# Second scan pass: vn copied ahead of vs behind the fifth level's copies, output sums issued behind the fourth level's mask

## The chip, the cores and the metric

One core of a Trainium2 chip runs the whole program. The metric is the device time of one execution in microseconds (us). Three executions of the kernel before gave 2560.66, 2562.65 and 2566.15 us; the median is 2562.65.

## The reference

One layer of a flow-matching backbone: a modulated RMS norm, then side by side a gated DeltaNet in both directions (4 heads of 128) and a gated spatial MLP, one input and one output projection, a residual add, and a squared-ReLU MLP. 128 context tokens and 2048 latent tokens are computed. The change touches the DeltaNet scan of the second (backward) direction. Cut to what matters:

```python
def gated_delta_chunked(q, k, v, g, beta, s0):
    ...
    a_mat = jnp.where(strict, jnp.einsum('bnhcd,bnhsd->bnhcs', k_beta, k) * decay, 0.0)
    sol = lax.linalg.triangular_solve(a_mat + jnp.eye(DN_CHUNK, dtype=f32), rhs,
                                      left_side=True, lower=True, unit_diagonal=True)
    ...
    def step(S, xs):
        qd, kd, u_c, w_c, qk_c, gl = xs
        v_new = u_c - jnp.einsum('bhck,bhkv->bhcv', w_c, S)
        o = jnp.einsum('bhck,bhkv->bhcv', qd, S) + jnp.einsum('bhcs,bhsv->bhcv', qk_c, v_new)
        S = S * jnp.exp(gl)[..., None, None] + jnp.einsum('bhck,bhcv->bhkv', kd, v_new)
        return S, o

def delta_bidir(q, k, v, g2, beta2, s0):
    o_f, s_f = gated_delta_chunked(q, k, v, g2[:, :, 0], beta2[:, :, 0], s0[:, 0])
    ...
    return o_f + flip(o_b), jnp.stack([s_f, s_b], axis=1)

def mixer(h, s0, n_chunks, w_in_l, conv_l, a_log_l, dt_bias_l, o_norm_l, ws_l, bs_l, w_out_l):
    proj = h @ w_in_l
    ...
    o_a = rmsnorm(o_a, o_norm_l) * jax.nn.silu(gate.reshape(B, T, H_A, DV))
    ...
    return out @ w_out_l, s_new
```

## The kernel before

The program has five stages on TensorE (PE). An input projection runs to about 490 us. A first (forward) scan pass over 17 chunks of 128 tokens, units 0 to 16, ends at about 860. The second (backward) pass, units 17 to 33, follows to about 1205 (one unit is about 21 us). Then come the two products of the MLP. Large products are made of three reduced-precision products each, lines L241, L242 and L243 (a high and a low part of each operand).

A unit has two halves. Its **prep** inverts a triangular matrix of 128 by 128 for each of four heads: from the loaded tiles KK and QK it makes AH (ACT, L1080) and X, and then goes through five levels s = 2, 4, 8, 16, 32. A level is a product AH·Y (L1109), a mask on VectorE (DVE) that makes P (L1113), a pair of products (L1122, L1124), and copies of Y and X on ScalarE (ACT, L1125 and L1126). Behind the second level's copies stands QK times the decay E (DVE, L1129). Then the two blocks of 64 are joined (L1141, copy P on ACT L1142, L1148 and L1150), and a last correction gives R (DVE, L1162) and T (ACT, L1171). The prep of one unit runs ahead of its scan, and two units' levels interleave.

The **scan** has four steps, written with a helper quad() that issues four products, one for each head (all at L1026):

1. S·kT into vt (DVE, L1183); S·qT into o (ACT, L1175);
2. T·vt into a PSUM tile p; vs = p times a column (DVE, L1196); vn = p (ACT, L1198);
3. vs·kt, and S updated from it (DVE, L1212);
4. vn·QK, and two output sums: o from o and the forward pass's output of (DVE, L1231), then o plus the product (DVE, L1233).

The output o is then normed (ACT L1363; DVE L1366 to L1371, called rr and o in the trace) and transposed on PE (L1384, o and the spatial half ob) into oH (ACT, L1387) and oL (DVE, L1388). The output projection, the **fills**, is 48 products for each unit: 24 for each half n of the columns, in PSUM tiles pj or pm. At its end stand tmp (DVE, L1407) and x + tmp (DVE, L1408), and for t > 8 further steps for the MLP (norm, transposes L888, stores from opH and opL, L902 to L909).

What runs when is set by a list of events with times in units; sorted by time, they issue their instructions. Each engine's queue is in that order but for what a scheduler may move. Two rules constrain it: emit() ties each fill behind the fourth last event of a chain or prep, and calm() ties the DVE and ACT instructions of a function behind the last instruction that level_done() has marked on their engine (on DVE the masks and the join's Y, on ACT the copies of X):

```python
        def level_done(n):
            x = tc.nc.cur_bb.bb.instructions[-1]
            urgent[x.engine].append(x)
        def calm(f, lag=0):
            start = here()
            f()
            for x in tc.nc.cur_bb.bb.instructions[start:]:
                if x.engine in urgent and len(urgent[x.engine]) > lag:
                    tc.add_manual_dep(x, urgent[x.engine][-1 - lag].name, ...)
```

All DMAs of the pass are issued by SyncE (SP) in one queue: loads (KK L1031, QK L1035 by qk_load, kt and vt L1043, kT and qT L1041) and stores. QK has three buffers; the PSUM tiles pd of prep and scan rotate through four.

Of the kernel before, what the change touches and what calls it, by code (L numbers as in the profile page):

```python
# [13 lines left out]
ALU = mybir.AluOpType  # L14
# [7 lines left out]
NT = 17  # L22
# [21 lines left out]
BT = 1  # L44
# [20 lines left out]
def hybrid_step(  # L65
# [7 lines left out]
    V, A, G, T = nc.vector, nc.scalar, nc.gpsimd, nc.tensor  # L73
# [137 lines left out]
    def here():  # L211
        return len(tc.nc.cur_bb.bb.instructions)
# [82 lines left out]
    with ExitStack() as ph:  # L295
# [496 lines left out]
        for bi in range(len(BLOCKS)):  # L792
# [6 lines left out]
            at = {e: n for n, e in enumerate(order)}  # L799
            tile_of = {}  # L800
            for n, (gi, h) in enumerate(order):
                u = us[n] if bi == 0 and n < 3 else feature_tile(blk, bi, gi, h)
# [157 lines left out]
    with ExitStack() as ph:  # L960
# [8 lines left out]
        def pd():  # L969
            return psd.tile([P, 4, P], F32, tag="d", name="pd", bufs=4)  # L970
# [10 lines left out]
        def q32(tag, bufs=1, pool=None):  # L981
            return (pool or dl).tile([P, 4, P], F32, tag=tag, name=tag, bufs=bufs)
# [24 lines left out]
# [6 lines that stand above are left out]
                    tc.add_manual_dep(x, urgent[x.engine][-1 - lag].name, mybir.DependencyInfo(  # L1013
                        mybir.DependencyClass.NoSync, mybir.DependencyReason.DATA), reason="order")

        def unit(t, d):

            u = {}
# [5 lines left out]
            def quad(p, lhs, rhs):  # L1024
                for h in range(H):
                    T.matmul(p[:, h, :], lhs[:, h, :], rhs[:, h, :], start=True, stop=True)  # L1026
# [21 lines left out]
            @prep.append  # L1048
            def _():
                e = s32("E")  # L1050

                def decay():
                    for h in range(H):
                        A.activation(e[:, h, :], u["gb"][:, h, :], AF.Abs, scale=-1.0, bias=col(gcol, h))
                    A.activation(e, e, AF.Exp, scale=-1.0)

                calm(decay, 2) if d else decay()
                es = s32("Es")
                G.affine_select(out=es, in_=e, pattern=[[0, 4], [-sg, P]], compare_op=ALU.is_gt, fill=0.0,
                                base=0, channel_multiplier=sg)  # L1060
                G.affine_select(out=e, in_=e, pattern=[[0, 4], [sg, P]], compare_op=ALU.is_ge, fill=0.0,
                                base=0, channel_multiplier=-sg)
                u["Es"], u["E"] = es, e
# [126 lines left out]
            @scan.append  # L1190
            def _():
                p = pd()
                quad(p, u["T"], u["vt"])
                u["vs"] = q32("vs", 1)
                cols = eglg[:, t, d * 4 : d * 4 + 4].unsqueeze(2).to_broadcast([P, 4, P])
                V.tensor_tensor(out=u["vs"], in0=p, in1=cols, op=ALU.mult)  # L1196
                u["vn"] = q32("vn", BT)
                A.copy(u["vn"], p)  # L1198

            @scan.append  # L1200
            def _():
# [16 lines left out]
            @scan.append  # L1218
            def _():
                p = pd()  # L1220
                quad(p, u["QK"], u["vn"])
                of = u["of"].rearrange("p (h d) -> p h d", h=H) if d else None
                if u["s"] is None:
                    u["o"] = o = q32("o", 2)
                    if d == 0:
                        A.copy(o, p)
                    else:
                        V.tensor_tensor(out=o, in0=p, in1=of, op=ALU.add)
                else:
                    o = u["o"]  # L1230
                    V.scalar_tensor_tensor(out=o, in0=o, scalar=-0.5, in1=of if d else p, op0=ALU.mult, op1=ALU.add)  # L1231
                    if d:
                        V.tensor_tensor(out=o, in0=o, in1=p, op=ALU.add)  # L1233
                if d == 0:
                    store(out=of_d[t * P : (t + 1) * P, :].rearrange("p (h d) -> p h d", h=H), in_=o)

# [108 lines left out]
        def o_loads(u):  # L1345
            t = u["t"]
            u["of"], u["ga"] = w512("of"), w512("ga")
            load(out=u["of"], in_=of_d[t * P : (t + 1) * P, :])
            load(out=u["ga"], in_=gate_d[t * P : (t + 1) * P, :])
# [74 lines left out]
        def at(time, fn, kind=None):  # L1424
            events.append((time, len(events), fn, kind))

        def spread(t0, t1, steps, kind):
            for j, st in enumerate(steps):
                at(t0 + (t1 - t0) * (j + 0.5) / len(steps), st, kind)

        def scan_step(i, f):
            def g():
                u = units[i]
                if "s" not in u:
                    u["s"] = None if i in (0, NT) else units[i - 1]["sn"] if i not in (1, NT + 1) else u["s0"]
                f()
            return g

        def after(i):

            d = 0 if i == 0 else 1
            store(out=new_state[0, 0, d].rearrange("h k v -> k h v"), in_=units[i]["sn"])

        def state_load(i):

            s0 = fpart("s0").rearrange("p (h d) -> p h d", h=H)
            load(out=s0, in_=state_delta[0, 0, 0 if i == 0 else 1].rearrange("h k v -> k h v"))
            units[i + 1]["s0"] = s0

        def noted(name, f):  # L1450

            start = here()
            f()
            done[name] = tc.nc.cur_bb.bb.instructions[start:]

        def after_weights(f, names, engines):

            start = here()
            f()
            for name in names:  # L1460
                behind(name, start, engines)

        p2, p3 = WINDOWS[:8], WINDOWS[8:]
        for i, u in enumerate(units):
            w = p2 if i <= NT else p3
            at(i - 3 if i > 1 else -12.1, lambda i=i, u=u: noted(("kk", i), u["prep_loads"]))
            at(i - 3 if i > 1 else -11.1, lambda i=i, u=u: after_weights(
                u["qk_load"], (("kk", 1),) if i < 2 else (), (mybir.EngineType.SP,)))
            at(i - 1, lambda i=i, u=u: after_weights(u["scan_loads"], LATER.get(i, ()), (mybir.EngineType.SP,)))
            u["prep"][:2] = [lambda i=i, f=f: after_weights(f, AHEAD_OF.get(i, ()), (mybir.EngineType.Activation,  # L1470
                                                                                    mybir.EngineType.DVE))
                             for f in u["prep"][:2]]
            n = len(u["prep"])
            for j, st in enumerate(u["prep"]):
                at(i - w[0] + (j + 0.5) * (w[0] - w[1]) / n if i or j > 9 else -11.6 if j < 2
                   else 0.2 * j - 8.15, st, "prep")
            for j, f in enumerate(u["scan"]):
                behind_join = 0.12 if j == 2 and i > NT else 0.0
                at(i + w[2] + (w[3] - w[2]) * (j + 0.5) / 4 + behind_join, scan_step(i, f), "chain")
            if i in (0, NT):  # L1480
                at(i - 1, lambda i=i: state_load(i))
                at(i + w[2] + (w[3] - w[2]) * 0.7, lambda i=i: after(i))
            if i >= NT:
                at(i, lambda u=u: o_loads(u))
                first, second = o_steps(u)
                spread(i + p3[4], i + p3[5], first, "fill")
                spread(i + p3[6], i + p3[7], second, "fill")
                if u["t"] > 8:
                    st = h2_steps(u["t"], pj, fraw, w512, fpart, fhalf, lambda u=u: u["x2"])
                    spread(i + p3[8], i + p3[9] + 0.2, st[:5], "fill")  # L1490
                    spread(i + p3[9] + 0.2, i + p3[9] + 2.1, [lambda f=f: calm(f) for f in st[5:]], None)
# [73 lines left out]
    def add(out, a, b, op=ALU.add):  # L1565
        V.tensor_tensor(out=out, in0=a, in1=b, op=op)  # L1566
# [199 lines left out]
    def sums(i, k, r):  # L1766
        if i == 1:
            add(r[0], r[1], r[0], ALU.subtract)
            store(out=t_d[5, k], in_=r[0])
            add(r[1], r[2], r[1], ALU.subtract)  # L1770
            store(out=t_d[7, k], in_=r[1])
        elif i == 5:
            add(r[1], r[1], r[0], ALU.subtract)
            store(out=t_d[6, k], in_=r[1])
        else:
            add(r[0], r[0], r[1], ALU.subtract)
            store(out=t_d[4, k], in_=r[0])
# [192 lines left out]
    for j, t in enumerate(range(8, -1, -1)):  # L1970
        st = h2_steps(t, bank, lambda: w512("junk"), w512)
        p = 10 + 19 * j // 2
# [7 lines left out]
    for p, (o, n, b) in enumerate(seq):  # L1980
        u = units[n]
# [130 lines left out]
```

## Time and profile before

| what | us |
|---|---|
| median of 3 executions | 2562.65 |
| profiled execution, its time | 2561.29 |
| profiled execution, span of the trace | 2559.5 |
| PE busy | 2531.2 |
| DVE busy | 1829.7 |
| ACT busy | 1258.6 |
| DMA queue of all loads and stores, mean share of 16 engines | 70.3% |

The granted clock of TensorE is 0.999 over the run. The span is the trace from its first to its last instruction; "idle" in a view is the time in which an engine waited before a line, with what released it. The chain of work that ended last is PE for 88% of the span, DMA 5%, DVE 4% and ACT 2%. For a short wait in a stage with a PE that is almost always busy, the waits of PE and the timeline of that stage are the views to use.

### The profile page before, as it was taken

To read this page: it belongs to the slowest core of one execution; us is meant where nothing else is said; L and a number is where in the kernel's file an instruction comes from. 1 tells how busy PE (TensorE), PEld (TensorE's weight loads), DVE (VectorE), ACT (ScalarE), POOL (GpSimd) and SP (SyncE) were. 2 spreads that over 40 slices of the span, in tenths; PEclk is the share of its full clock that TensorE was granted. 3 is DMA by queue.
4 is the path that set the end of the run, shared out by engine and by line. 5 is a ranking of instruction groups with operands and counts; after the bars stand their busy time and mean duration, and the time that the engine had idled before them with its cause. 6 is when DMAs were issued, how large, how long until landed. Compare 5 with 4: busy or idle time off the path is not lost.

```text
span 2559.5 us, 44412 instructions
## 1 busy us (share of the span) xinstructions
PE 2531.2 (99%) x15268; PEld 2135.2 (83%) x15268; DVE 1829.7 (71%) x3790; ACT 1258.6 (49%) x3119; POOL 228.2 (9%) x448
## 2 busy tenths in 40 slices
PE   9999999999999999999999999999999999999998
PEld 5999999788888788788888888888888888888887
DVE  5867746776666878886678877777675557784875
ACT  4755556554554767763455544444342433243442
POOL 3112212211101111110000000000000000000000
PEclk9999999999999999999999999999999999999999
DMA  8977747744445657785867789665489979786673
GB/s 286 308 222 207 210 120 230 261 155 153 149 145 161 210 176 256 263 302 190 304 207 233 241 286 348 191 180 172 145 272 371 340 265 327 251 262 208 225 261 110
DMA packets 503912, 588.66 MB, mean 230 GB/s; under 512 B 36148, under 2 KB 298588, under 8 KB 500102
## 3 DMA queue, kind: packets, MB, share of 16 engines
q1 hardware_dynamic: 503686, 585.82, 70.3%
q8 instruction: 120, 1.97, 0.3%
q14 instruction: 106, 0.87, 0.1%
HBM read 406.01 MB, written 179.67 MB: 229 GB/s over the span
## 4 chain that ended last, share of the span: by engine, by line
PE 88%; DMA 5%; DVE 4%; ACT 2%; issue 1%; SPq 0%; POOL 0%; POOLq 0%; DVEq 0%; ACTq 0%
PE f L241 16%; PE f L243 16%; PE f L242 16%; PE pj L241 7%; PE pj L243 7%; PE pj L242 7%; PE pd L1026 5%; PE pm L241 2%; PE pm L243 1%; PE pm L242 1%; PE pt L625 1%; DMA raw<-in_w_mod_dram 1%; PE pt L584 1%; DMA QK<-qk_d 1%; DMA raw<-in_w_ff_dram 1%
## 5 line engine op out<-in xcount | busy, mean ns | idle before, releaser
L241 PE MATMUL f<-hop,zH 128*128 128x512 f32 (+1 forms) x976 | 376.2, 386 | 1.2 <-ACT zH L1572 1.2
L242 PE MATMUL f<-hop,zH 128*128 128x512 f32 (+1 forms) x976 | 376.1, 386 | 0.0
L243 PE MATMUL f<-hop,zL 128*128 128x512 f32 (+1 forms) x976 | 376.1, 386 | 0.0
L241 PE MATMUL f<-hop,wH 128*128 128x512 f32 x896 | 349.5, 391 | 1.2 <-ACT p L1645 1.0
L242 PE MATMUL f<-hop,wH 128*128 128x512 f32 x896 | 348.7, 389 | 0.0
L243 PE MATMUL f<-hop,wL 128*128 128x512 f32 x896 | 347.1, 389 | 0.0
L1572 ACT CAST zH<-zraw 128x512 fp32r<-128x512 f32 x240 | 146.9, 620 | 294.6 <-DMA zraw<-s_d 89.6
L241 PEld LDWEIGHTS f<-hop,zH 128*128 128x128 f32 x976 | 183.4, 188 | 38.6 <-ACT zH L1572 1.8
L243 PEld LDWEIGHTS f<-hop,zL 128*128 128x128 f32 x976 | 183.4, 188 | 37.0 <-DVE zL L1566 0.4
L242 PEld LDWEIGHTS f<-hop,zH 128*128 128x128 f32 x976 | 183.4, 188 | 36.9 <-issue 0.2
L1566 DVE TENSOR_TENSOR zL<-zraw,zH 128x512 fp32r<-128x512 f32 x240 | 163.0, 687 | 66.9 <-ACT zH L1572 51.5
L241 PEld LDWEIGHTS f<-hop,wH 128*128 128x128 f32 x896 | 168.2, 188 | 36.8 <-ACT p L1645 2.0
L243 PEld LDWEIGHTS f<-hop,wL 128*128 128x128 f32 x896 | 168.2, 188 | 35.2
L242 PEld LDWEIGHTS f<-hop,wH 128*128 128x128 f32 x896 | 168.3, 188 | 34.5
L241 PE MATMUL pj<-kH,wH 128*128 128x386 f32 (+2 forms) x568 | 190.6, 338 | 1.7 <-ACT junk L601 1.1
L243 PE MATMUL pj<-kH,wL 128*128 128x386 f32 (+2 forms) x568 | 189.7, 335 | 0.0
L242 PE MATMUL pj<-kL,wH 128*128 128x386 f32 (+2 forms) x568 | 189.4, 335 | 0.0
L184 POOL TENSOR_TENSOR r<-rsq,nhalf 128x1 f32<-128x1 f32 (+1 forms) x37 | 23.4, 634 | 1380.4 <-DVE rsq L183 1380.4
L571 DVE SCALAR_TENSOR_TENSOR cv<-pj,vec,cv 128x384 f32<-128x384 f32 (+2 forms) x164 | 86.9, 539 | 52.4 <-ACT cv L568 51.0
L1572 ACT CAST wH<-s 128x512 fp32r<-128x512 f32 x96 | 59.4, 621 | 123.3 <-DVE s L1566 116.9
L241 PEld LDWEIGHTS pj<-kH,wH 128*128 128x128 f32 x568 | 107.1, 189 | 5.1 <-issue 2.4
L202 DVE TENSOR_TENSOR wL<-raw,wH 128x512 fp32r<-128x512 f32 x120 | 81.2, 684 | 38.6 <-ACT wH L201 35.5
(423 smaller groups left out, 5788.1 us busy)
## 6 DMA issues: line engine op xcount, KB each, us to landing
zraw<-z_d SPq DMA_DIRECT2D x212, 256.0 KB
raw<-in_w_ff_dram SPq DMA_DIRECT2D x192, 256.0 KB
hop<-hop_d SPq DMA_DIRECT2D x28, 1024.0 KB
z_d<-c SPq DMA_DIRECT2D x96, 256.0 KB
zraw<-s_d SPq DMA_DIRECT2D x96, 256.0 KB
raw<-in_w_mod_dram SPq DMA_DIRECT2D x80, 256.0 KB
r<-in_w_ff_dram SPq DMA_DIRECT2D x80, 256.0 KB
s_d<-s SPq DMA_DIRECT2D x64, 256.0 KB
```

The costliest lines, as they stand in the source:

```text
L184: G.tensor_tensor(out=out, in0=t[:np_, :n], in1=nhalf[:np_, :n], op=ALU.pow)
L202: V.tensor_tensor(out=lo, in0=raw, in1=f32(h), op=ALU.subtract)
L241: T.matmul(ps, lh, rh, start=first and i == 0, stop=False, skip_group_check=more)
L242: T.matmul(ps, lh, rl, start=False, stop=False, skip_group_check=more)
L243: T.matmul(ps, ll, rh, start=False, stop=last and i == n - 1, skip_group_check=more)
L571: V.scalar_tensor_tensor(out=cv[:, o : o + m], in0=ps[:, s + sh : s + sh + m], scalar=convw[:, w, j : j + 1], in1=cv[:, o : o + m], op0=AL ...
L584: T.transpose(pq[:, i * P : (i + 1) * P], u["x2"][:, i * P : (i + 1) * P], ident)
L625: T.matmul(ps[:, i * P : (i + 1) * P], kTt[:, i * P : (i + 1) * P], rhs[:, i * P : (i + 1) * P], start=True, stop=True)
L1026: T.matmul(p[:, h, :], lhs[:, h, :], rhs[:, h, :], start=True, stop=True)
L1566: V.tensor_tensor(out=out, in0=a, in1=b, op=op)
L1572: A.copy(h, src)
```

## The change

Three edits, all on the second pass (d = 1). In the scan's second step vn is now made before vs, and with calm(), so behind the last marked copy of X. In the fourth step the two output sums stand in a function and are tied with calm(), behind the last marked mask. The scan's events are issued a little later: the second step by 0.1 units, the third by 0.12 (as before), the fourth by 0.03.

```diff
@@ scan, step 2 @@
+                u["vn"] = q32("vn", BT)
+                if d:
+                    calm(lambda: A.copy(u["vn"], p))
                 V.tensor_tensor(out=u["vs"], in0=p, in1=cols, op=ALU.mult)
-                u["vn"] = q32("vn", BT)
-                A.copy(u["vn"], p)
+                if d == 0:
+                    A.copy(u["vn"], p)
@@ scan, step 4 @@
-                    V.scalar_tensor_tensor(out=o, in0=o, scalar=-0.5, in1=of if d else p, op0=ALU.mult, op1=ALU.add)
-                    if d:
-                        V.tensor_tensor(out=o, in0=o, in1=p, op=ALU.add)
+
+                    def sums():
+                        V.scalar_tensor_tensor(out=o, in0=o, scalar=-0.5, in1=of if d else p, op0=ALU.mult,
+                                               op1=ALU.add)
+                        if d:
+                            V.tensor_tensor(out=o, in0=o, in1=p, op=ALU.add)
+
+                    calm(sums) if d else sums()
@@ events @@
-                behind_join = 0.12 if j == 2 and i > NT else 0.0
-                at(i + w[2] + (w[3] - w[2]) * (j + 0.5) / 4 + behind_join, scan_step(i, f), "chain")
+                shift = {1: 0.1, 2: 0.12, 3: 0.03}.get(j, 0.0) if i > NT else 0.0
+                at(i + w[2] + (w[3] - w[2]) * (j + 0.5) / 4 + shift, scan_step(i, f), "chain")
```

The lines behind the edits have larger numbers in the kernel after: vs is L1199 there (L1198 is vn in both), S's update L1215, the sums L1236 and L1239, the o copies L1395 and L1396, and tmp and x + tmp are L1415 and L1416.

The next rows are ACT's order in unit 26, before. An 8x32 form of Y and X is the fifth level's pair of copies (two rows), and E, fraw and opH belong to other steps.

```order
1119 L1054 ACTIVATE E<-gb,gcol 128x128 x4
1120 L868 ACTIVATE fraw,ss_15495<-x 128x512
1121 L1055 ACTIVATE E<-E 128x512
1122 L1198 COPY vn<-pd 128x512
1123 L1387 CAST oH<-pj 128x512
1124 L1125 CAST Y<-pd 128x8x32
1125 L1126 CAST X<-pd 128x8x32
1126 L1125 CAST Y<-pd 128x64x4
```

The same place on ACT, after:

```order
1122 L1054 ACTIVATE E<-gb,gcol 128x128 x4
1123 L1055 ACTIVATE E<-E 128x512
1124 L1395 CAST oH<-pj 128x512
1125 L1125 CAST Y<-pd 128x8x32
1126 L1126 CAST X<-pd 128x8x32
1127 L1198 COPY vn<-pd 128x512
1128 L1125 CAST Y<-pd 128x64x4
1129 L1126 CAST X<-pd 128x64x4
```

vn has moved behind oH and the fifth level's copies, and ahead of those of the next unit's second level.

On DVE in the same unit, before (P with sm_186 is the fifth level's mask; opL and y belong to the MLP's steps; the numbers count the rows of the queue from the program's start):

```order
1356 L1129 TENSOR_TENSOR QK<-QK,E 128x512
1357 L1408 TENSOR_TENSOR x<-x,tmp 128x512
1358 L1366 TENSOR_TENSOR r_16639<-rq 128x4
1359 L1231 SCALAR_TENSOR_TENSOR o<-o,of 128x512
1360 L1369 SCALAR_TENSOR_TENSOR rr<-rr,rq 128x4
1361 L1371 SCALAR_TENSOR_TENSOR o<-o,rr,ga 128x128 x4
1362 L1113 TENSOR_TENSOR P_5794<-pd,sm_186 128x8x32
1363 L1113 TENSOR_TENSOR P_5791<-pd,sm_183 128x64x4
1364 L904 TENSOR_TENSOR opL<-y,opH 128x512
1365 L909 TENSOR_TENSOR y<-y 128x512
1366 L1196 TENSOR_TENSOR vs<-pd,eglg 128x512
1367 L1071 SCALAR_TENSOR_TENSOR KK<-KK,beta,Es 128x128 x4
```

The same stretch of DVE's queue after:

```order
1361 L1374 TENSOR_TENSOR r_16639<-rq 128x4
1362 L1129 TENSOR_TENSOR QK<-QK,E 128x512
1363 L1377 SCALAR_TENSOR_TENSOR rr<-rr,rq 128x4
1364 L1379 SCALAR_TENSOR_TENSOR o<-o,rr,ga 128x128 x4
1365 L1113 TENSOR_TENSOR P_5794<-pd,sm_186 128x8x32
1366 L1113 TENSOR_TENSOR P_5791<-pd,sm_183 128x64x4
1367 L909 TENSOR_TENSOR y<-y 128x512
1368 L904 TENSOR_TENSOR opL<-y,opH 128x512
1369 L1396 TENSOR_TENSOR oL<-pj,oH 128x512
1370 L1071 SCALAR_TENSOR_TENSOR KK<-KK,beta,Es 128x128 x4
1371 L1199 TENSOR_TENSOR vs<-pd,eglg 128x512
```

vs has moved behind oL and KK. The add of x and tmp (now two rows ahead of this piece) and r have moved ahead of QK, and the first output sum is gone from here. It now stands here, some ten rows sooner, between the masks of the fourth level (sm_185) and of the next unit's first (sm_182):

```order
1349 L1113 TENSOR_TENSOR P_5793<-pd,sm_185 128x16x16
1350 L1236 SCALAR_TENSOR_TENSOR o<-o,of 128x512
1351 L904 TENSOR_TENSOR opL<-d,opH 128x512
1352 L881 TENSOR_SCALAR x<-x,r 128x512 x2
1353 L1239 TENSOR_TENSOR o<-o,pd 128x512
1354 L1113 TENSOR_TENSOR P_5790<-pd,sm_182 128x128x2
```

Before, only the second sum (o<-o,pd) stood in that stretch, ahead of both masks.

On PE the products vn·QK of the same unit stand before between the last correction (L1159, L1160) and the fills:

```order
9086 L1159 MATMUL pd<-Y,AH 128x128
9087 L1160 LDWEIGHTS AL
9088 L1160 MATMUL pd<-Y,AL 128x128
9089 L1026 MATMUL pd<-vn,QK 128x128 x4
9090 L241 MATMUL pj<-wH,oH 128x512
9091 L242 MATMUL pj<-wL,oH 128x512
9092 L243 MATMUL pj<-wH,oL 128x512
```

After, the last of four L1109 and six fills come first (the other three L1109 stand ahead of this piece):

```order
9094 L1109 MATMUL pd<-Y,AH 128x64
9095 L241 MATMUL pj<-wH,oH 128x512
9096 L242 MATMUL pj<-wL,oH 128x512
9097 L243 MATMUL pj<-wH,oL 128x512
9098 L241 MATMUL pj<-wH,oH 128x512
9099 L242 MATMUL pj<-wL,oH 128x512
9100 L243 MATMUL pj<-wH,oL 128x512
9101 L1026 MATMUL pd<-vn,QK 128x128 x4
9102 L1109 LDWEIGHTS AH
```

vn·QK has moved behind four products of L1109 and six fills. T·vt has moved likewise, behind six fills, the transposes of o and the fifth level's products.

SP's queue around the load of QK for unit 28, before (x is a half of the input row for the residual add, hop a store of the MLP's input, h and y a block of it):

```order
751 L894 DMA h_12_d<-ev 128x512
752 L906 DMA hop_7_d<-opH 128x512
753 L1380 DMA x<-in_x_sample_dram 128x512
754 L1035 DMA QK<-qk_d 128x512
755 L906 DMA hop_7_d<-opL 128x512
756 L1380 DMA x<-in_x_sample_dram 128x512
757 L1041 DMA kT<-kT_d 128x512
```

And after:

```order
751 L894 DMA h_12_d<-ev 128x512
752 L906 DMA hop_7_d<-opH 128x512
753 L1388 DMA x<-in_x_sample_dram 128x512 x2
754 L906 DMA hop_7_d<-opL 128x512
755 L1035 DMA QK<-qk_d 128x512
756 L1041 DMA kT<-kT_d 128x512
```

The load of QK has moved behind the second x and the store of opL.

## The prediction

> **What bounds the kernel now.** I read the busy shares first, then busy time by stage, then the waits of PE in the stage that changes, and last the timeline around its two longest waits. The rows are the engine line of the page and the stretches of the pass that is edited (start and end, length, PE, PEld, DVE, ACT and POOL busy with their instructions, clock, DMA share, GB/s).
>
> ```profile
> PE 2531.2 (99%) x15268; PEld 2135.2 (83%) x15268; DVE 1829.7 (71%) x3790; ACT 1258.6 (49%) x3119; POOL 228.2 (9%) x448
> 887.00:1108.00 221.00, 214.45 (x1940) 178.43 (x1939) 183.79 (x465) 162.08 (x502) 38.52 (x51) 1.00 0.70 235
> 1108.00:1205.00 97.00, 96.99 (x827) 81.83 (x827) 73.89 (x180) 53.53 (x171) 10.15 (x11) 1.00 0.72 247
> ```
>
> PE is the bound: 2531.2 of 2559.5 us. The second pass lies at about 860 to 1205 us. The edit acts from unit 18 on (its test is i > NT; the new order of vn and vs, with test d, from unit 17), whose moved products begin at about 887. From there to 1108 PE is idle for 221.00 - 214.45 = **6.55 us**, and behind 1108 for 0.01. The change neither adds nor removes a matrix product, so this is about all that it can gain. PE's waits there, by the program's lines (total, times, longest):
>
> ```profile
> PE pd L1141 <- ACT Y L1125: 2.2, 2, 1.4
> PE pj L241 <- DVE tmp L1407: 1.6, 2, 0.8
> PE pd L1109 <- ACT Y L1125: 0.8, 1, 0.8
> PE pm L1384 <- DVE ug L1264: 0.5, 1, 0.5
> PE pm L241 <- DVE tmp L1407: 0.4, 2, 0.2
> PE pd L1122 <- DVE vt L1183: 0.4, 1, 0.4
> PE pd L1026 <- DVE o L1233: 0.2, 1, 0.2
> PE pd L1148 <- ACT P L1142: 0.2, 1, 0.2
> ```
>
> They add up to 6.3 us. The longest, twice, is the join of the 64-blocks, L1141, behind the fifth level's copy Y on ACT. The timeline of unit 26 shows why (start, length, engine, line, and in brackets the idle time before with its releaser):
>
> ```profile
> 1056.64 0.28 PE L1124 MATMUL pd<-X,P 128*128 128x64 f16 x4
> 1058.26 0.68 DVE L1196 TENSOR_TENSOR vs<-pd,eglg 128x512 f32<-128x512 f32 x1
> 1058.97 0.59 ACT L1198 COPY vn<-pd 128x512 f32<-128x512 f32 x1 [2.92 <-DVE vs L1196]
> 1059.45 0.59 ACT L1387 CAST oH<-pj 128x512 fp32r<-128x512 f32 x1
> 1059.93 0.39 ACT L1125 CAST Y<-pd 128x256 f16<-128x256 f32 x1
> 1060.37 0.28 PE L1141 MATMUL pd<-Y,AH 128*128 128x64 f16 x4 [1.35 <-ACT Y L1125]
> 1060.68 0.68 DVE L1407 TENSOR_TENSOR tmp<-pm,row 128x512 f32<-128x512 f32 x1
> 1061.42 0.50 PE L241 MATMUL pm<-wH,oH 128*128 128x512 f32 x1 [0.18 <-DVE tmp L1407]
> ...
> ACT vn L1198 <- DVE vs L1196: 17.2, 12, 3.0
> ```
>
> ACT stands for 2.92 us at vn, since vs reads the same PSUM tile and DVE comes to it late. oH and Y, which the join needs, are queued behind vn. Over the pass (890 to 1200) this is 17.2 us of ACT in 12 waits, but only two of them reach PE.
>
> DVE's long wait is for QK, the first row here; the next five are work behind it, and the last is DVE's sum of these waits:
>
> ```profile
> 1052.63 0.69 DVE L1129 TENSOR_TENSOR QK<-QK,E 128x512 f32<-128x512 f32 x1 [2.75 <-DMA QK<-qk_d]
> 1053.24 0.68 DVE L1408 TENSOR_TENSOR x<-x,tmp 128x512 f32<-128x512 f32 x1
> 1053.91 0.68 DVE L1231 SCALAR_TENSOR_TENSOR o<-o,of 128x512 f32<-128x512 f32 x1
> 1054.51 0.15 DVE L1369 SCALAR_TENSOR_TENSOR rr<-rr,rq 128x4 f32<-128x4 f32 x1
> 1066.13 1.12 DVE L1212 SCALAR_TENSOR_TENSOR S<-S,egl,pd 128x128 f32<-128x128 f32 x4
> 1067.38 0.69 DVE L1162 SCALAR_TENSOR_TENSOR R<-pd,two 128x512 f16<-128x512 f32 x1
> ...
> DVE QK L1129 <- DMA QK<-qk_d: 20.6, 12, 2.7
> ```
>
> From QK at 1052.63 to the update of S, which ends at 1066.13 + 1.12 = 1067.25, DVE hardly pauses. S there is as late as QK was.
>
> **The change part by part.** Nothing is removed: instructions of the second pass change places on DVE, ACT, PE and SP.
>
> *vn behind the fifth level's copies, ahead of vs.* Y is then free of vs. The fifth level's products that it copies ended at 1056.64 + 0.28 = 1056.92, so Y can run about 2.5 us sooner than at 1059.93 even with oH ahead of it (0.59), more than the 1.35 us that PE waited. The join's two waits go: **-2.2 us**. Behind this join the fills of tile n = 1 stand behind the next level in units 24, 26 and 28, so the two short waits for tmp go too: **-0.4**. The two longer ones (pj, 1.6) are in units where the fills keep their place and stay.
>
> What is late next in unit 26 is S. PE comes 1.35 us sooner to the products L1109 that now stand ahead of vn·QK and take the PSUM tile that S's update frees. S does not come sooner: on DVE it stands behind the step on QK, a load whose place on SP moves as well.
>
> ```profile
> 1046.55 0.46 SPq L1380 DMA_DIRECT2D x<-in_x_sample_dram  x1
> 1047.11 0.90 SPq L1035 DMA_DIRECT2D QK<-qk_d  x1
> 1048.11 0.39 SPq L906 DMA_DIRECT2D hop_d<-opL  x1
> 1048.55 0.42 SPq L1380 DMA_DIRECT2D x<-in_x_sample_dram  x1
> ...
> SPq L1035 <- PE pd L1026: 8.0, 5, 2.4
> ```
>
> In this stretch the opL store and the second x, issued at 1048.11 and 1048.55 before, now come ahead of QK. A transfer of 128x512 f32, as in QK's row, is 256 KB. The window's row has 235 GB/s at a DMA share of 0.70, which is 336 GB/s at full share (an estimate), so two more of them ahead are 512 KB / 336 GB/s = 1.56 us. Against it, the first output sum (1053.91 to 1054.51, 0.60) and the add of x and tmp with a small instruction behind it (1053.24 to 1053.91, 0.67) now stand ahead of QK on DVE, in time that was idle: 1.27. The two nearly cancel, so S stays and the gain of unit 26 is given back: **+1.4**. Bounds: 0, and 2.2 if unit 28's join gives its share back as well.
>
> The Trainium skill, page "DMA: Bandwidth & Descriptors", section "Anatomy of one DMA", puts a transfer at a fixed 2.0 us and its bytes by 436 GB/s, which for 256 KB is an estimate of 2.6 us. The trace does not agree here: QK's issue ended at 1048.01 and DVE was released at 1052.63, 4.6 us later. [...]
>
> *vs behind vn.* vs now stands behind KK on DVE and waits for vn. Its reader is vs·kt. T·vt moves too, behind six fills, the transposes of o and the fifth level's products, which began at 1054.62 and ended where the next level's began, at 1056.76: 2.1 us.
>
> ```profile
> 1053.73 1.14 PE L1026 MATMUL pd<-vt,T 128*128 128x128 f32 x8
> 1054.62 0.48 PE L241 MATMUL pm<-wH,oH 128*128 128x512 f32 x1
> 1056.76 0.28 PE L1122 MATMUL pd<-P,X 128*128 128x64 f16 x4
> 1058.86 1.12 DVE L1071 SCALAR_TENSOR_TENSOR KK<-KK,beta,Es 128x128 f32<-128x128 f32 x4
> 1063.35 1.14 PE L1026 MATMUL pd<-vs,kt 128*128 128x128 f32 x8
> ```
>
> vs ended at 1058.94 and was read at 1063.35: 4.4 us of cover. T·vt's new end, about 1057, is no bound. Ahead of vs I put KK's 1.12 and vn's 0.59; 2.7 us are left. **0**; if the cover fell, 15 times what is missing.
>
> *Sums behind the fourth mask.* The two sums run sooner, in DVE time before QK that was idle. They free PSUM tiles that were freed by other instructions; S·qT's wait of 0.2 for L1233 goes (**-0.2**), and R·X and L1109 get new holders. A wait that the trace does not have: 0 if all are in time, 3.0 if each of 15 units waits as S·qT once did; most have a run of fills between, so I take **+1.0**.
>
> *Shorter runs of fills.* By the order of instructions PE's fills fall into 166 runs instead of 156. The first product of a run is the dearer:
>
> ```profile
> 1064.94 0.48 PE L241 MATMUL pm<-wH,oH 128*128 128x512 f32 x1
> 1065.26 0.39 PE L242 MATMUL pm<-wL,oH 128*128 128x512 f32 x1
> 1065.49 0.39 PE L243 MATMUL pm<-wH,oL 128*128 128x512 f32 x1
> ```
>
> From start to start 0.32 against 0.23: 10 x 0.09 = **+0.9**.
>
> *vn·QK behind four L1109 and six fills.* Four such f16 products took 1056.76 - 1056.64 = 0.12, so this is 0.12 + 6 x 0.23 + 0.09 = 1.6 us later. Its cover is that the next QK load is delayed by the queue anyway; the price without that is the second rival.
>
> **Sum:** -2.2 - 0.4 - 0.2 + 1.4 + 1.0 + 0.9 = **+0.5 us**. The profiled execution took 2561.29 us (span 2559.5), 1.36 below the median of the three runs, 2562.65. Since the measured time is a median, the forecast is 2562.65 + 0.5 = 2563.15, given as **2563.2**: within 0.2% (5.1 us), which is about what a measurement of this kernel can tell from no change.
>
> **The rivals.**
>
> *ACT's freedom pays in full (faster).* No unit is held by S, and all waits of the table go, tmp's and L1109's included. For it speaks that they share the queue with vn. Against it: the two longer waits for tmp stand where the fills keep their place, and ug is not touched by the change. It gives -6.55 + 0.9 = -5.65, so 2557.0.
>
> *QK's load follows vn·QK (slower).* Five QK loads waited on SP for a matrix product at L1026 (8.0 us, up to 2.4). If these are late by the 1.6 us that vn·QK moves, and DVE passes it on through S to the next vn·QK, the pass goes at the loop's pace: 5 x 1.6 = 8.0, with the runs' 0.9 and the join's -2.8 it is +6.1, so 2568.8. It decides where the delay in the issue is longer than the queue of transfers behind which QK would have stood; DVE's work cut ahead of QK speaks against it. [...]
>
> *The change does not do what it says (the same).* If DVE, not vs, sets when Y is ready, the waits stay and only the runs cost: +0.9, 2563.6.
>
> **How the numbers follow.** Forecast 0.62, no effect 0.10, both within 0.2%; full gain 0.17; loop 0.11. The forecast's own ends are 2562.65 - 2.8 + 0.9 = 2560.8 (nothing given back) and 2562.65 - 2.8 + 0.9 + 2.2 + 3.0 = 2565.95. The range takes in the first rival at its price and the second up to just below its own, **2556.5 to 2568.5**; about 0.2 lies outside. Faster 0.17, same 0.72, slower 0.11.
>
> **What would show it.** Right: no wait of vn for vs, L1141's wait gone from both places, vs waiting for vn instead, QK's waits on DVE about as long, a new wait of L1109 for S near 1066. Wrong: PE idle between 887 and 1108 below 2 us (the first rival), or QK's waits on DVE and SP clearly above 20.6 and 8.0 us with PE idle in units 24 to 28 (the second). Most of all the forecast hangs on the 1.4 us that S is to take back, and on the holders of PSUM tiles, whose waits no row of before shows.

## The result and the profile after

| kernel | median, us | runs | ratio to before | 95% interval |
|---|---|---|---|---|
| before | 2562.69 | 7 | | |
| after | 2571.70 (2566.76 to 2575.32) | 7 | 1.0033 | 1.0024 to 1.0042 |

The change is slower by 9.0 us, 3.2 us above the top of the range. Its profiled execution took 2571.7 us (span 2569.6, granted clock 0.999). The first pass is untouched: S·kT ahead of unit 19 starts at 898.1 us for 897.9 before, and the first product of the MLP comes 8.3 us later (1236.9 for 1228.6). So the loss is made in the second pass, unit by unit: that S·kT starts 0.2 us later than before, the one of the last unit 8.0.

The same two stretches as before, by engine (same columns):

```profile
887.00:1108.00 221.00, 213.86 (x1914) 176.59 (x1911) 181.22 (x456) 160.57 (x495) 37.80 (x49) 1.00 0.69 230
1108.00:1205.00 97.00, 94.86 (x806) 77.59 (x804) 74.90 (x177) 53.68 (x173) 10.17 (x13) 1.00 0.68 224
```

PE is idle for 7.14 and 2.14 us where it was idle for 6.55 and 0.01, and in the same 221 us it starts 26 products fewer (1914 for 1940). PE's waits from 887 us on, after:

```profile
PE pd L1148 <- ACT P L1142: 2.5, 3, 0.9
PE pd L1122 <- DVE P L1113: 1.8, 3, 0.6
PE pj L1392 <- DVE o L1379: 1.6, 2, 1.2
PE pd L1109 <- ACT Y L1125: 0.8, 1, 0.8
PE pd L1109 <- ACT X L1126: 0.8, 2, 0.5
PE pm L1392 <- DVE o L1379: 0.7, 2, 0.4
PE pd L1141 <- ACT Y L1125: 0.4, 1, 0.4
PE pd L1109 <- DVE S L1215: 0.3, 1, 0.3
PE pm L241 <- DVE tmp L1415: 0.2, 1, 0.2
```

The joins' wait for Y (L1141) fell from 2.2 to 0.4 and those for tmp from 2.0 to 0.2, as the change would have it. In their place stand waits that before did not have: at the transposes of o (L1392, was L1384) for its scaling on DVE, 2.3 us; at the fifth level (L1122) for the mask, 1.8; behind the join (L1148) for the copy P, 2.5 for 0.2. All rows of the list add up to 9.1 us, for 6.3 before. That is 2.8 of the 9.0 us; the rest is below.

ACT's wait of vn for vs (17.2 us) is gone; vn now waits for its product only. DVE's wait for QK is hardly longer (21.5 us for 20.6), while SP's queue waits far longer ahead of QK's load (16.2 us with both of its releasers on PE, for 9.6). From the views of waits of ACT, DVE and SP, 890 to 1205 (SP from 880):

```profile
ACT vn L1198 <- PE pd L1026: 1.4, 5, 0.3
...
DVE QK L1129 <- DMA QK<-qk_d: 21.5, 12, 3.6
...
SPq L1035 <- PE pd L1109: 15.4, 5, 4.0
SPq L1035 <- PE pd L1026: 0.8, 2, 0.4
```

Before, the second row of QK's load on SP, beside the 8.0 us of the prediction's row, was:

```profile
SPq L1035 <- PE pd L1109: 1.6, 4, 0.6
```

The timeline of unit 26 shows how the new waits hang together. First before: vn·QK of the unit before, then from o's scaling to the fifth level:

```profile
1043.95 1.11 PE L1026 MATMUL pd<-vn,QK 128*128 128x128 f32 x8
...
1054.70 1.14 DVE L1371 SCALAR_TENSOR_TENSOR o<-o,rr,ga 128x128 f32<-128x128 f32 x4
1055.86 0.39 PE L243 MATMUL pm<-wH,oL 128*128 128x512 f32 x1
1056.09 0.60 PE L1384 MATMUL pj<-ident,o 128*128 128x128 f32 x4
1056.53 0.28 PE L1122 MATMUL pd<-P,X 128*128 128x64 f16 x4
```

and after, from the same vn·QK and the load of QK on:

```profile
1049.09 1.05 PE L1026 MATMUL pd<-vn,QK 128*128 128x128 f32 x8
...
1051.90 0.40 SPq L906 DMA_DIRECT2D hop_d<-opL  x1
1052.39 0.42 SPq L1035 DMA_DIRECT2D QK<-qk_d  x1
...
1058.56 0.69 DVE L1129 TENSOR_TENSOR QK<-QK,E 128x512 f32<-128x512 f32 x1 [3.31 <-DMA QK<-qk_d]
1058.57 0.40 PE L243 MATMUL pm<-wH,oL 128*128 128x512 f32 x1
1059.17 0.15 DVE L1377 SCALAR_TENSOR_TENSOR rr<-rr,rq 128x4 f32<-128x4 f32 x1
1059.36 2.00 DVE L1379 SCALAR_TENSOR_TENSOR o<-o,rr,ga 128x128 f32<-128x128 f32 x4
1060.19 0.33 PE L1392 MATMUL pj<-ident,o 128*128 128x128 f32 x1 [1.22 <-DVE o L1379]
1060.89 0.85 PE L1392 MATMUL pj<-ident,o 128*128 128x128 f32 x3 [0.38 <-DVE o L1379]
1061.28 0.74 DVE L1113 TENSOR_TENSOR P<-pd,sm 128x256 f16<-128x256 f32 x2
1061.74 0.28 PE L1122 MATMUL pd<-P,X 128*128 128x64 f16 x4
```

Before, o's scaling ended at 1054.70 + 1.14 = 1055.84 and PE came to the transposes at 1056.09: a margin of **0.25 us**. After, PE could have come at 1058.57 + 0.23 = 1058.80, and the scaling ended at 1059.36 + 2.00 = 1061.36.

Take the start of vn·QK of the unit before as zero (1043.95 before, 1049.09 after). PE is due at the transposes 12.1 us behind it in the kernel before and 9.7 us in the kernel after. Of these 2.4 us, 1.6 is the place of vn·QK itself, moved back behind L1109 and six fills, and the rest is T·vt, which no longer lies between. The end of o's scaling stays at 11.9 and 12.3 us, since it stands on DVE behind the step on QK, whose load is issued behind that vn·QK: in units 22, 23, 25, 27 and 29 0.03 to 0.05 us behind its end in both kernels, in unit 28, shown here, 2.05 and 2.25 us behind it, after other DMAs of SP. So both shifts eat one margin, and there was 0.25 us of it. From L243 to the fifth level's first product PE now takes 3.17 us (1058.57 to 1061.74) where it took 0.67 (1055.86 to 1056.53): 2.5 us in this one place.

Of that 2.5 the view of waits names 1.6. The profile models a product's end, and where PE stops between the products of a group it counts busy time: PE's busy sum rose by 6.4 us (2531.2 to 2537.6) for the same 15268 products. Over all units, PE's stops ahead of the transposes of o, between them and behind them at the fifth level, added up from start to start beyond the usual distance, are 7.6 us after and 0 before; the view names 4.1 of the 7.6. These 3.5 us, ten more runs of fills, and one wait of 1.0 us for a load at the MLP's start are what I can name of what the list leaves out of the 9.0.

### The profile page after: what moved, and what is told of

It reads as the page before. It is cut to its first block, busy times and chain, and to the rows that moved or that the text cites. A ratio compares the mean times of both kernels' runs of the same rounds, so it can differ in the third digit from the quotient of the medians.

```text
span 2569.6 us, 44452 instructions
## 1 busy us (share of the span) xinstructions
PE 2537.6 (99%) x15268; PEld 2135.0 (83%) x15268; DVE 1832.7 (71%) x3790; ACT 1260.5 (49%) x3119; POOL 229.2 (9%) x448
## 5 line engine op out<-in xcount | busy, mean ns | idle before, releaser
L243 PE MATMUL f<-hop,zL 128*128 128x512 f32 (+1 forms) x976 | 376.3, 386 | 0.0
L243 PE MATMUL f<-hop,wL 128*128 128x512 f32 x896 | 347.5, 389 | 0.0
L243 PEld LDWEIGHTS f<-hop,zL 128*128 128x128 f32 x976 | 183.3, 188 | 37.8 <-DVE zL L1574 1.0
L243 PEld LDWEIGHTS f<-hop,wL 128*128 128x128 f32 x896 | 168.2, 188 | 35.4
L243 PE MATMUL pj<-kH,wL 128*128 128x386 f32 (+2 forms) x568 | 189.7, 335 | 0.0
```

What stands on the lines that cost most here:

```text
L243: T.matmul(ps, ll, rh, start=False, stop=last and i == n - 1, skip_group_check=more)
```

## Experiments

Times are medians; the difference in us is to the kernel before, run beside it on the same chip. An interval of the ratio is about 0.0009 to either side, 2.3 us.

**The two new shifts apart.** Each is the changed kernel with a shift taken out, or before with the shifts alone.

```diff
-                shift = {1: 0.1, 2: 0.12, 3: 0.03}.get(j, 0.0) if i > NT else 0.0
+                shift = {2: 0.12}.get(j, 0.0) if i > NT else 0.0              # no_shift13
+                shift = {2: 0.12, 3: 0.03}.get(j, 0.0) if i > NT else 0.0     # no_shift1
+                shift = {1: 0.1, 2: 0.12}.get(j, 0.0) if i > NT else 0.0      # no_shift3
```

> After, with only the old shift of the third step (0.12): the new order of vn and vs and the tied sums stay, the second and fourth step go back to their old times, so T·vt stands again ahead of the six fills and the transposes, and vn·QK right behind the last correction. If the two shifts carry the loss (either theory A or B), the time is that of the kernel before or up to 3 us less, 2560 to 2563, and PE no longer waits at the transposes L1392 for the scaled o (4.5 us in the changed kernel). If the new order on ACT and DVE itself costs (theory C), it stays above 2567 and the waits at the transposes remain.

2567.47, +4.9, ratio 1.0019 (1.0010 to 1.0028).

> After, without the shift of the second step (0.1): T·vt stands ahead of the six fills and the transposes again, vn·QK stays late. Theory A (T·vt moved away leaves PE about 1 us early at the transposes of o, whose scaling DVE has not done): the waits at L1392 and at the masks of level 5 behind them go, and the time falls by 5 or more, to 2566 or less. Theory B (late vn·QK delays the loads of QK, and DVE with them): within 2 us of the changed kernel, 2570 to 2573, with the waits at L1392 still there.

2564.23, +1.7, ratio 1.0005 (0.9997 to 1.0014). PE's named waits at the transposes are down to 1.0 us, and those for the mask are gone.

> After, without the shift of the fourth step (0.03): vn·QK stands right behind the last correction, T·vt stays behind the transposes. Theory B (late vn·QK): QK's loads are issued about 1.6 us sooner, the step on QK comes sooner, the waits at L1392 go, and the time falls by 5 or more to 2566 or less. Theory A (T·vt): 2570 to 2573, and the waits at L1392 stay above 3 us.

2567.58, +5.0, ratio 1.0019 (1.0010 to 1.0028). The waits at the transposes are down to 0.3, those for the mask to 1.1.

> Before, with the new shifts alone (0.1, 0.12, 0.03), vn behind vs as before and the sums not tied. If the shifts carry the whole loss and the new order of vn and the sums neither gains nor loses: 2570 to 2573. If the new order gains what it should at the joins (2 to 3 us), this is slower than the changed kernel, 2573 to 2576. If the new order carries part of the loss (theory C), it is nearer to before, 2563 to 2568.

2566.02, +3.4, ratio 1.0013 (1.0003 to 1.0022), the shifts of the change in the kernel before.

Either shift taken out takes most of the wait at the transposes away, as the margin above says: neither theory A nor B alone. From start to start, the stops around the transposes go from 7.6 us to 2.5 in no_shift1, 3.4 in no_shift3 and 0 in no_shift13. But my picture that the shifts carry everything fell with no_shift13: without them the change still costs 4.9 us.

**The two new orders apart, and the step on QK.** vn_only and sums_only have the first or the second edit of the change alone; the other two tie the step on QK of the second pass behind a later mask, in the changed kernel and in before:

```diff
-                    if s == 2:
-                        V.tensor_tensor(out=u["QK"], in0=u["QK"], in1=u["E"], op=ALU.mult)
+                    if s == (4 if d else 2):
+                        qk = lambda: V.tensor_tensor(out=u["QK"], in0=u["QK"], in1=u["E"], op=ALU.mult)
+                        calm(qk) if d else qk()
```

> Before, with the first edit alone: vn made before vs and tied behind the fifth level's copy of X; sums and shifts as before. The two new orders together (without the new shifts) gave 2567.5, 4.9 above before. If vn's place carries it (vs late behind vn and KK, S and all behind it late): 2566 to 2568. If the sums carry it: 2561 to 2563, with the join's wait for Y at L1141 (2.2 before) gone.

2558.89, **-4.5**, ratio 0.9981 (0.9972 to 0.9990). PE's waits from 887 to 1205 in this kernel:

```profile
PE pd L1148 <- ACT P L1142: 1.4, 3, 0.9
PE pm L1387 <- DVE ug L1267: 0.5, 1, 0.5
PE pd L1141 <- ACT Y L1125: 0.4, 1, 0.4
PE pd L1026 <- DVE S L1215: 0.3, 1, 0.3
PE pd L1109 <- DVE ug L1318: 0.3, 1, 0.3
```

2.9 us for 6.3: the joins and tmp no longer wait where they did (the 0.4 at L1141 is at 889.5, in another unit), and S, the fourth row, takes back only 0.3.

> Before, with the second edit alone: the two output sums tied behind the mask. If the sums carry the 4.9 us of the two new orders (the first sum now stands ahead of vt on DVE, and P2 and X wait on PE): 2566 to 2568, with waits of L1122 for vt and of L1089 for X. If vn's place carries them: 2561 to 2564.

2565.71, +2.3, ratio 1.0006 (0.9997 to 1.0015): unclear, and not a gain. The waits that were expected are hardly there: 0.3 us of L1122 for vt, none of L1089 for X.

> After, with the step on QK (L1129) of the second pass tied behind the second level's... next mask (s = 4) instead of at s = 2, so that on DVE the scaling of o and the fifth level's mask no longer stand behind the load of QK. Theory B (DVE stands before QK, and PE then waits at the transposes for o and at level 5 for the mask, 7.5 us together): these waits go and the time falls by 5 or more, to 2566 or less. Theory A (PE merely comes earlier to the transposes, and o's scaling is late by its own chain of squares, power and scale): 2569 to 2573, waits at L1392 still above 3 us.

2560.96, -2.4, ratio 0.9993 (0.9984 to 1.0001), and **10.7 below the changed kernel** by medians (11.4 by differences to before) with the whole change in it. PE's order of instructions is that of the changed kernel but for a few fills and transposes. Its waits from 887 on are now only these, 1.5 for 9.1:

```profile
PE pd L1109 <- ACT Y L1125: 0.8, 1, 0.8
PE pd L1142 <- ACT Y L1125: 0.4, 1, 0.4
PE pd L1149 <- ACT P L1143: 0.3, 1, 0.3
```

The timeline of unit 26 in it, DVE and PE:

```profile
1051.91 0.16 DVE L1378 SCALAR_TENSOR_TENSOR rr<-rr,rq 128x4 f32<-128x4 f32 x1 [0.93 <-POOL rr L184]
1052.11 1.14 DVE L1380 SCALAR_TENSOR_TENSOR o<-o,rr,ga 128x128 f32<-128x128 f32 x4
1053.17 0.75 DVE L1113 TENSOR_TENSOR P<-pd,sm 128x256 f16<-128x256 f32 x2
1053.83 0.68 DVE L1129 TENSOR_TENSOR QK<-QK,E 128x512 f32<-128x512 f32 x1
...
1054.54 0.60 PE L1393 MATMUL pj<-ident,o 128*128 128x128 f32 x4
1054.97 0.28 PE L1122 MATMUL pd<-P,X 128*128 128x64 f16 x4
```

o's scaling ends at 1053.25, 1.3 us before PE comes, the masks stand ready, and the step on QK begins without a wait. PE's stops around the transposes are 0.1 us in all units for 7.6. T·vt and vn·QK are as late as in the changed kernel: with the sums tied as the change ties them, what they cost, they cost through the one instruction on DVE that waits for a load while work that PE needs is queued behind it.

> Before, with the same move of the step on QK behind the mask at s = 4. If DVE's wait for QK (20.6 us) is what makes vs late and so the join's Y: DVE's wait falls below 10 us, L1141's two waits (2.2) go, and the time is 2559 to 2562. If QK's load is only late because everything else is, nothing moves: 2562 to 2564.

2559.63, **-3.7**, ratio 0.9987 (0.9978 to 0.9995). DVE's wait for QK and the join's for Y are gone from the lists.

**Sums and shifts with vn in its new place, and with the step on QK late.** after_no_sums is the changed kernel with the sums issued as before; the other three combine the edits.

> After, with the output sums no longer tied behind the mask (they are issued as in the kernel before); vn's place and the shifts stay. vn alone gave 2558.9 and both new orders without new shifts 2567.5. If the tied sums are what spoils vn's gain: at least 4 us below the changed kernel, 2567 or less, and less waiting of PE at the transposes for o. If the shifts spoil it by themselves (T·vt and vn·QK late): 2569 to 2573.

2569.85, +6.5, ratio 1.0032 (1.0019 to 1.0044).

> Before, with vn ahead of vs (the first edit) and the step on QK behind the mask at s = 4, no tied sums and no new shifts. If both gains come from different waits (vn -4.5, the step on QK -3.7): 2555 to 2557. If both remove the same one, vs made late by the load of QK and Y late behind it: 2558 to 2560.

2558.04, **-5.3**, ratio 0.9983 (0.9974 to 0.9992): no more than vn alone within the intervals, so the two remove mostly the same wait.

> After, with the sums not tied and the step on QK behind the mask at s = 4. If the shifts cost only by the load of QK on DVE, this is as fast as vn with the late step on QK, within 2 us. If the earlier arrival of PE at the transposes costs in itself: 3 or more above it, 2560 to 2564.

2564.36, +1.0, ratio 1.0006 (0.9997 to 1.0015). The shifts cost 6.3 us against vn_qk_late though QK is out of the way. It is not PE's earlier arrival at the transposes: PE has no named wait there, and 0.3 us of stops from start to start. What grew is DVE's wait at the second output sum, which stands ahead of a mask, for the product of the late vn·QK. The first row is of vn_qk_late, the second of this kernel, 890 to 1205:

```profile
DVE o L1237 <- PE pd L1026: 1.3, 5, 0.3
DVE o L1240 <- PE pd L1026: 7.9, 9, 1.5
```

The same wait is 7.5 to 8.0 us in the three other kernels with a late vn·QK and sums that are not tied (shift_only, after_no_sums, vn_shift3), and 3.2 to 3.5 where they are tied (after, no_shift1, after_qk_late). So a late vn·QK has a second path, and the tie of the sums shortens it. That this wait makes up the 6.3 us is not shown.

> After, without the new shifts and with the step on QK behind the mask at s = 4. The same without the late step on QK was 2567.5. If the tied sums cost because DVE's later work stands behind the load of QK: 2557 to 2562. If the two sums ahead of vt cost by themselves (L1122 waiting for vt, L1089 for X): 2564 to 2568.

2561.50, -1.9, ratio 0.9995 (0.9986 to 1.0004), where it was +4.9 with the step on QK in its old place: 6.8 us by that one instruction.

**Which shift spoils vn, and what makes QK's load late.** vn_shift1 and vn_shift3 add one of the two new shifts to vn_only; the last has another buffer for QK:

```diff
-        identq = f16("identq")
-        V.tensor_copy(identq, bc4(ident16))
...
-                u["QK"] = q32("QK", 3)
+                u["QK"] = q32("QK", 2, dl if t % 2 else pp)
```

> Before, with vn ahead of vs and the shift of the second step alone (0.1): T·vt moves behind six fills, the transposes of o and the fifth level; vn·QK stays. vn alone gave 2558.9, vn with both new shifts 2569.9. Theory A (T·vt away lets PE reach the transposes about 1 us before o is scaled): 2565 or more, with waits at the transposes (L1384 in before) for o. Theory B (only the late vn·QK matters): 2557 to 2561.

2562.09, -0.3, ratio 1.0001 (0.9992 to 1.0010).

> Before, with vn ahead of vs and the shift of the fourth step alone (0.03): vn·QK moves behind four products of L1109 and six fills, T·vt stays. Theory B (QK's buffer is released later, its load comes later, and DVE with it): 2565 or more, with DVE's wait for QK at or above that of vn alone (18.2 us). Theory A: 2557 to 2561.

2562.46, +0.1, ratio 1.0002 (0.9993 to 1.0010).

Each takes back the gain of vn, 4.2 and 4.6 us; both together (after_no_sums) cost 11.0. Neither theory was right alone. In both kernels PE stops at the fifth level, behind the transposes, for the mask (2.2 and 1.7 us from start to start, 0 in vn_only) and not at the transposes themselves; vn_shift3 also has the longer wait at the second output sum (7.9 us for 1.3).

> Before, with vn ahead of vs and four buffers for QK instead of three (two of them in the pool of prep; a constant tile of 1 KB is left out for the space and its source read in its place), so that the load of QK no longer waits for vn·QK of three units before. Its DVE order differs too: the step on QK comes behind KK. If DVE waits for QK only because its buffer is released late: DVE's wait for the load (18.2 with vn alone) falls below 5 us, and the time is that of vn with the late step on QK, 2556 to 2560. If the queue of transfers makes it late: the wait stays above 10 us.

2559.88, -2.5, ratio 0.9991 (0.9982 to 1.0000). DVE's wait for the load is gone from its list altogether; the longest that is left, of 890 to 1205:

```profile
DVE P L1111 <- PE pd L1107: 13.1, 12, 2.4
```

But the step on QK also stands elsewhere on DVE in this kernel, right behind KK: for unit 28 some 14 us sooner, counted from vn·QK of unit 25, than in vn_only. So its time does not tell the buffer from the place. That the load can be had in time with a fourth buffer is shown: it is issued one unit (about 21 us) sooner, and in units 22 to 33 it is 10.6 to 14.3 us from issue to use. That this alone would have mended the changed kernel is not shown, and was not tried with the old place on DVE.

**The sums without the shifts.** Why vn and the sums together are at +4.9, where vn alone is at -4.5, shows on DVE in no_shift13 (timeline of unit 23 to 24, and PE's waits from 887):

```profile
987.21 0.69 DVE L1129 TENSOR_TENSOR QK<-QK,E 128x512 f32<-128x512 f32 x1 [1.64 <-DMA QK<-qk_d]
...
987.89 1.12 DVE L1183 SCALAR_TENSOR_TENSOR vt<-pd,neg,vt 128x128 f32<-128x128 f32 x4
...
1001.13 0.69 DVE L1236 SCALAR_TENSOR_TENSOR o<-o,of 128x512 f32<-128x512 f32 x1
...
1002.46 1.12 DVE L1215 SCALAR_TENSOR_TENSOR S<-S,egl,pd 128x128 f32<-128x128 f32 x4
1003.50 0.42 DVE L1081 TENSOR_TENSOR X<-AH,bd 128x512 f16<-128x512 f16 x1
```

```profile
PE pd L1148 <- ACT P L1142: 2.2, 2, 2.0
PE pd L1122 <- DVE vt L1183: 2.1, 2, 1.1
PE pd L1089 <- DVE X L1081: 1.7, 3, 0.8
```

The tie only gives the sums an earliest place. Where vn·QK comes early, the first sum slips in ahead of S and of X, and PE waits at L1089 for X; vt, behind the step on QK, makes PE wait at L1122. With the fourth step's shift (no_shift1) both are smaller and the time is 3.2 us less: the same shift that costs 4.6 us on vn alone. The parts do not add. That these waits are all of the sums' price is argued from the rows, not shown by a run.

## Why the prediction was wrong, point by point

*What bounds, and the size of what can be gained*: right. vn_only removes 3.4 us of named waits and gains 4.5 us of the 6.55. Most signs that I had set for a right forecast appeared as well: vn no longer waits for vs, the join's two waits are gone, QK's wait on DVE is about as long. None of them looked at the transposes.

*vn ahead of vs, -2.2 and -0.4*: right in mechanism and too small. Both joins' and nearly all of tmp's waits went (also the two at pj that I left standing), and alone it gives -4.5.

*+1.4 taken back by S*: wrong. S holds PE for 0.3 us in the changed kernel and in vn_only.

***T·vt behind six fills and the transposes, 0***: the step that failed. I asked whether vs would still be in time for vs·kt, and it was. I did not ask what PE reaches sooner when 0.89 us of products (1053.73 to 1054.62) are taken out ahead of it. It reaches the transposes of o, where before the margin was 0.25 us. On top of vn, this shift alone costs 3.2 to 4.2 us (vn_shift1 against vn_only, by medians and by differences to before), and taken out of the changed kernel it gives back 7.4 (no_shift1, +1.7 for +9.0).

***vn·QK 1.6 us later, hidden by the queue***: failed in the same place. I held that the load of QK stands behind transfers anyway, and that this hides the delay. It did not: the load shown went from 5.5 us, issue to use (1047.11 to 1052.63), to 6.2 (1052.39 to 1058.56), and the twelve loads of units 21 to 33 for which DVE waited from 5.0 to 4.6 on average, 0.4 us less where hiding needs 1.6. So a later issue was, for the most part, a later landing. Taken out of the changed kernel, this shift gives back 4.0 (no_shift3, +5.0). The Trainium skill's "DMA: Bandwidth & Descriptors", section "Anatomy of one DMA — SWDGE (gpsimd) path", has the fit from which the prediction took its estimate of 2.6 us, for a DMA that GpSimd issues. On SP's queue the load of unit 22 agrees with it (2.54 us, 916.53 to 919.07, at a DMA share of 0.51 from 912 to 920); the one of unit 28 does not (5.52, at 0.95 from 1042 to 1053). The second rival came nearest, 2568.8 for 2571.7. Of its signs SP's was there (16.2 us ahead of QK for 9.6) and DVE's was not (21.5 for 20.6, not clearly above), and its path was not the one I gave: not DVE, S and the next vn·QK, but DVE, the scaling of o and the masks. So the nearness of its price is in part luck.

*Sums behind the mask, +1.0 and -0.2*: under-priced. I took the first sum's new place for idle time of DVE. Alone they cost +2.3 (not clear of nothing), and with vn in place 9.4 (no_shift13, +4.9, against vn_only, -4.5). I looked at what the sums leave, not at what stands behind them where they arrive.

*Fills of n = 1 behind the next level, counted as -0.4*: the fills were also the cover of the copy P behind the join. L1148's wait rose from 0.2 to 2.5 us in the units 22, 24 and 26. With the step on QK tied later and almost the same order of PE (after_qk_late) 0.3 is left; without the shifts (vn_sums_qk_late) 1.9 is, so it is not that step alone.

*Ten more runs of fills, +0.9*: not measured by itself.

The forecast took eight terms as if they added up. The runs give vn -4.5, shifts +3.4, sums +2.3, which add up to +1.2. That this is near the forecast's +0.5 is luck: none of the three measured parts has the size that I gave it. The change as a whole is at +9.0. What is missing is that all three meet at one instruction: DVE standing at QK, 3.3 us in unit 26, with o's scaling and the masks queued behind it, and in no_shift13 vt too. Moving that one instruction takes 10.7 us off, and makes the same change a kernel that is 2.4 us below before (interval 0.9984 to 1.0001, so not clear of no change). The version to keep is vn ahead of vs alone, 2558.9, or with the step on QK late, 2558.0; both are clear of before, and not of each other.

Still open: whether DVE's wait at the second output sum is all of the 6.3 us that the shifts cost against vn_qk_late, and of the 3.4 that the tied sums bring back there; how much of the 9.0 is the place of vs behind KK; and the price of the runs of fills.

## What to carry to other kernels

When a step is moved later, look not only at who reads its result but at what its engine now reaches sooner, and at that instruction's margin in the trace before; 0.25 us is none. In this kernel the instruction that waits for a load belonged behind the work that the bounding engine needs, not ahead of it: the wait itself (20.6 us on an engine that is 71% busy) looked harmless until something came due behind it. Edits that pull work towards one place have to be priced together there.

## What the runs showed of the hardware that was not expected

On one queue, loads of 256 KB took from 2.5 to 6.9 us from issue to use in the kernel before (units 21 to 33, the twelve for which DVE waited). The shortest was issued into a lull, with nothing else issued on the queue for 2.8 us (unit 22):

```profile
916.53 0.32 SPq L1035 DMA_DIRECT2D QK<-qk_d  x1
919.07 0.69 DVE L1129 TENSOR_TENSOR QK<-QK,E 128x512 f32<-128x512 f32 x1 [0.26 <-DMA QK<-qk_d]
```

PE's stops between the products of one group appear as busy time, which is part of the 6.4 us more busy for the same products. So a comparison of start times (3.17 us for 0.67 at one place) shows a wait of 2.5 that the idle column gives as 1.6.
